# Gate and up of a SwiGLU layer as 2x2 block products, three of eight pairs of k tiles by seven products in place of eight

## The chip, the cores and the metric

The kernel runs on one core of a Trainium2 chip. The metric is device time in microseconds (us) of one execution, as a median of runs. Below, PE is TensorE (matmul), PEld its weight load, DVE is VectorE, ACT is ScalarE, POOL is GpSimd and SP is SyncE, which issues the transfers (DMAs).

## What is computed

The reference is a trunk of two layers over 256 tokens with a width of 2048. Each layer is a mixer (attention and recurrence, or pooling and attention), a residual with layer norm, a SwiGLU feed-forward part of hidden width 5632, and again a residual with layer norm. All is fp32. The change lies in the feed-forward part:

```python
def swiglu(x, w_gate, w_up, w_down):
    return (jax.nn.silu(x @ w_gate) * (x @ w_up)) @ w_down

for layer in range(2):
    y = ab_mixer(x, ...) if layer % 2 == 0 else cd_mixer(x, ...)   # each ends in "@ w_out"
    x = layer_norm(DN_ALPHA * x + y, ln_mix_g[layer], ln_mix_b[layer])
    f = swiglu(x, ffn_w_gate[layer], ffn_w_up[layer], ffn_w_down[layer])
    x = layer_norm(DN_ALPHA * x + f, ln_ffn_g[layer], ln_ffn_b[layer])
```

## The kernel before

**A product in three matmuls.** Every fp32 operand is kept as two parts, high (`h`, `hi`) and low (`l`, `lo`), and a product of a 128x128 piece of x (the stationary operand) with 128 rows by 512 columns of a weight is three matmuls into one bank of PSUM (`mm3`, L240 to L243): low by high, high by high, high by low. The 256 tokens are two tiles of 128, and the contraction over 2048 is 16 k tiles.

**Weights.** They stream in as halves: 128 x 2 k tiles x 512 columns, 512 KB, one DMA on SP's queue into one of four buffers `raw` (`load_half`, L124). ACT copies the high part into `whi` (L103), DVE subtracts it from `raw` and has the low part in `wlo` (L104). `whi` and `wlo` take their slots in turn from a ring: six slots in a pool of their own, and five more in the layer's end (two in a pool `wx`, three in `f0` or `f1`), 11 in all. The two parts of a half feed 12 matmuls: two k tiles, two token tiles, three each.

**The feed-forward part** (`ffn`, L353). The hidden width is 11 chunks of 512. They go in three phases, PHASES = ((0, 1, 2), (3, 4, 5, 6), (7, 8, 9, 10)). In a phase each chunk has eight halves of gate for both token tiles into two banks `acc`, then eight halves of up into two more; ACT takes the silu of gate (`sil`, L367), DVE multiplies it by up (L374), and PE transposes the result in eight pieces (L100) that are split into `yTh` and `yTl` for the next product. Behind the chunks of a phase stand its down products: four column blocks, with DVE adding each into the residual `res` (L257, L259). The residual norm behind the last phase reads `gam` and `bet`, which are loaded (L328, L329) at the start of the feed-forward part.

**The order of the work.** The program is written out as above; a scheduler then fixes the order of every engine when the program is built, with priorities as hints. On the chip each engine works through its order and waits on semaphores. PSUM has eight banks, shared as three `acc`, two `tr` (transposes) and three `mx`.

Of the kernel before, what the change touches and what calls it, by code (L numbers as in the profile page):

```python
# [11 lines left out]
F32 = mybir.dt.float32  # L12
# [58 lines left out]

@with_exitstack
def trunk(ctx: ExitStack, tc: tile.TileContext, a, out):
# [7 lines left out]
    ps = ctx.enter_context(tc.tile_pool(name="ps", bufs=1, space=PSUM))  # L81
# [8 lines left out]
    def acc():  # L90
        return ps.tile([P, NCH], F32, tag="acc", name="acc", bufs=3)

    def trp():
        return ps.tile([P, NCH], F32, tag="tr", name="tr", bufs=2)

    def mxp():
        return ps.tile([P, NCH], F32, tag="mx", name="mx", bufs=3)
# [4 lines left out]
    def split(hi, lo, src):  # L102
        nc.scalar.copy(hi, src)  # L103
        nc.vector.tensor_tensor(lo, src, hi.bitcast(F32), op=sub)  # L104
# [5 lines left out]
    rings = [(wp, 6)]  # L110
# [10 lines left out]
    last_load = [None]  # L121
    first = [True]

    def load_half(src, between=()):  # L124
# [5 lines left out]
        with tc.high_priority(offset=400):  # L130
# [5 lines left out]
            for i in range(parts):  # L136
# [7 lines left out]
                with ExitStack() as order:  # L144
                    for ins in behind:
                        order.enter_context(tc.issue_after(ins))
                    split(hi[:, s, :], lo[:, s, :], raw[:, s, :])
        return hi, lo

    def mm_chunk(halves, lhs, outs, tok_major=False, after=None, before=None):  # L150
# [8 lines left out]
        def mms(i, tok, pin=False):  # L159
            hi, lo = loaded[i]  # L160
            k0 = halves[i][1]
            for kk in range(2):
                xh, xl = lhs(tok, k0 + kk)
# [62 lines left out]
    def transpose4(src, hi, lo):  # L226
# [4 lines left out]
        split(hi, lo, v)  # L231
# [19 lines left out]
    def residual_tools(res, gam, bet, betT):  # L251
        stats = [sm.tile([P, 4, 6], F32, tag=f"st{t}", name=f"st{t}", bufs=1) for t in range(NT)]
# [82 lines left out]
    def out_proj(w, order, groups, res, gb):  # L335
        evac, norm = residual_tools(res, *gb)
        lhs = y_lhs(groups)
        xT = new_xT()
        for n in range(4):
            outs = [acc() for _ in range(NT)]  # L340
            halves = [(w[n, 2 * g + i], 4 * g + 2 * i) for g in order for i in range(2)]
# [11 lines left out]
    def ffn(fp, layer, xT, res, gb, last):  # L353
        evac, norm = residual_tools(res, *gb)
        lhs = x_lhs(xT)
        new = None if last else new_xT
        nxt = [None]
        for pi, chunks in enumerate(PHASES):
            groups = {}
            for c in chunks:  # L360
                first = pi == 0 and c == 0
                gouts = [acc() for _ in range(NT)]
                sil = {}

                def silu(tok):
                    sil[tok] = fp.tile([P, NCH], F32, tag="sil", name="sil", bufs=3)
                    nc.scalar.activation(sil[tok], gouts[tok], AF.Silu)  # L367

                mm_chunk([(a[f"gate{layer}"][c, i], 2 * i) for i in range(8)], lhs, gouts, tok_major=first, after=silu)
                uouts = [acc() for _ in range(NT)]  # L370
                groups[c] = new_yT()

                def gated(tok):
                    nc.vector.tensor_tensor(sil[tok], sil[tok], uouts[tok], op=mult)  # L374
                    s = slice(tok * P, (tok + 1) * P)
                    transpose4(sil[tok], groups[c][0][:, :, s], groups[c][1][:, :, s])

                mm_chunk([(a[f"up{layer}"][c, i], 2 * i) for i in range(8)], lhs, uouts, after=gated)
            end = pi == len(PHASES) - 1
            if end and not last:  # L380
                nxt[0] = new_xT()
            gl = [groups[c] for c in chunks]
            for n in range(4):
                outs = [acc() for _ in range(NT)]
                halves = [(a[f"down{layer}"][n, 2 * c + i], 4 * ci + 2 * i) for ci, c in enumerate(chunks) for i in range(2)]

                def after(tok):
                    with tc.high_priority(offset=1000 if end and n == 3 else 0):
                        evac(tok, n, outs[tok], pi == 0, end)
                        if end and n == 3:  # L390
                            norm(tok, nxt[0], out if last else None)

                mm_chunk(halves, y_lhs(gl), outs, tok_major=(end and n == 3), after=after)
        return nxt[0]
# [29 lines left out]
    def ab_mixer(mp, xT, yT):  # L424
# [239 lines left out]
        for c, ((kind, i), _) in enumerate(ab_plan()):  # L664
            outs = [acc() for _ in range(NT)]
            mm_chunk([(a["ab_in"][c, n], 2 * n) for n in range(8)], lhs, outs, before=load_x if c == 0 else None)
# [5 lines left out]
    def cd_mixer(mp, xT, yT):  # L672
# [118 lines left out]
        for c, (kind, _) in enumerate(cd_plan()):  # L791
            outs = [acc() for _ in range(NT)]
            mm_chunk([(a["cd_in"][c, n], 2 * n) for n in range(8)], lhs, outs, tok_major=(c == 0))
# [10 lines left out]
    with tc.tile_pool(name="ab", bufs=1) as mp:  # L804
        ab_mixer(mp, xT, yT)
# [4 lines left out]
    open_ring(ctx.enter_context(tc.tile_pool(name="wx", bufs=1)), 2)  # L810
    with tc.tile_pool(name="f0", bufs=1) as fp:
        open_ring(fp, 3)
        xT = out_proj(a["ab_out"], AB_OUT_GROUPS, yT, res, load_gb(fp, 0, "mix"))
        xT = ffn(fp, 0, xT, res, load_gb(fp, 0, "ffn"), False)
    rings.pop()
    yT = [new_yT() for _ in range(4)]
    with tc.tile_pool(name="cd", bufs=1) as mp:
        cd_mixer(mp, xT, yT)
    with tc.tile_pool(name="f1", bufs=1) as fp:
        open_ring(fp, 3)  # L820
        xT = out_proj(a["cd_out"], CD_OUT_GROUPS, yT, res, load_gb(fp, 1, "mix"))
        ffn(fp, 1, xT, res, load_gb(fp, 1, "ffn"), True)
# [54 lines left out]

def layout(i):
# [26 lines left out]
    for l in range(2):  # L905
        m[f"gate{l}"] = pieces(f["ffn_w_gate"][l])
        m[f"up{l}"] = pieces(f["ffn_w_up"][l])
# [24 lines left out]
```

## Time and profile before

| | |
|---|---|
| median of 3 runs | 2231.93 us (2229.7 to 2233.01) |
| the profiled execution, its own time | 2229.76 us |
| its span, first to last instruction | 2228.0 us |
| PE busy | 2201.6 us, 99% |
| DVE busy | 1313.6 us, 59% |
| ACT busy | 994.5 us, 45% |
| DMA queue of the weights | 418.94 MB, 57.4% of 16 engines |

The busy time of an engine is the time in which at least one instruction was at work, and says nothing of whether the others waited for it; that is read from the chain that ended last and from the list of waits.

### The profile page before, as it was taken

Reading aid. Unit: us, or ns where it says so; the run is one execution under the profiler, and the core shown is the slowest. Engines: PE = TensorE matmul, PEld = TensorE weight load, DVE = VectorE, ACT = ScalarE, POOL = GpSimd, SP = SyncE. Lnnn points to the kernel's source line nnn. Section 1 sums busy time; section 2 is a strip of 40 time slices with the busy share of each in tenths; the row PEclk is TensorE's granted clock in tenths of the full one; section 3 lists DMA queues with packets and bytes.
Section 4 is the critical chain, followed back from the end, with each engine's and each line's share of the span. In section 5 each row is a group of like instructions: output and inputs, shape, how many; then the busy total and the mean of one; then the engine's idle time right before and its main releaser. Section 6 shows DMA issues by size and latency. Waiting matters only on the chain.

```text
span 2228.0 us, 26810 instructions
## 1 busy us (share of the span) xinstructions
PE 2201.6 (99%) x10180; PEld 1833.9 (82%) x10180; DVE 1313.6 (59%) x1662; ACT 994.5 (45%) x1258; POOL 83.1 (4%) x67
## 2 busy tenths in 40 slices
PE   8999999999999999999999999999999999999997
PEld 7888888887888888888888788878888888888886
DVE  6886688667555545554455676665554554544454
ACT  6445544546443444344443564444444444444431
POOL 0010001002000000000000200020000000000001
PEclk9999999999999999999999999999999999999999
DMA  8555545676655556565656464656555555656562
GB/s 293 161 161 180 173 130 183 219 250 211 205 187 191 190 188 194 184 199 184 197 176 199 151 207 141 235 171 227 188 190 192 186 192 186 198 179 201 183 197 71
DMA packets 118898, 420.66 MB, mean 189 GB/s; under 512 B 14448, under 2 KB 17008, under 8 KB 117488
## 3 DMA queue, kind: packets, MB, share of 16 engines
q1 hardware_dynamic: 118768, 418.94, 57.4%
q8 instruction: 80, 1.31, 0.2%
q14 instruction: 50, 0.41, 0.1%
HBM read 416.78 MB, written 2.10 MB: 188 GB/s over the span
## 4 chain that ended last, share of the span: by engine, by line
PE 96%; DVE 2%; ACT 1%; DMA 0%; issue 0%; POOL 0%; DVEq 0%; ACTq 0%; POOLq 0%
PE acc L243 91%; PE tr L100 2%; PE mx L530 1%; PE mx L243 1%; DVE wlo L104 1%; DVE xTl L319 0%; PE mx L576 0%; PE mx L783 0%; ACT whi L103 0%; ACT res L288 0%; DVE res L274 0%; DMA raw<-in_cd_in 0%; DMA x<-in_xT 0%; DVE res L278 0%; PE mx L766 0%
## 5 line engine op out<-in xcount | busy, mean ns | idle before, releaser
L104 DVE TENSOR_TENSOR wlo<-raw,whi 128x1024 fp32r<-128x1024 f32 (+1 forms) x761 | 938.4, 1236 | 726.2 <-ACT whi L103 708.8
L103 ACT CAST whi<-raw 128x1024 fp32r<-128x1024 f32 (+1 forms) x761 | 800.6, 1053 | 987.4 <-PE acc L243 836.2
L243 PE MATMUL acc<-whi,xTl 128*128 128x512 f32 x2080 | 814.7, 394 | 13.7 <-DVE xTl L319 8.0
L243 PE MATMUL acc<-whi,xTh 128*128 128x512 f32 x2080 | 814.4, 392 | 0.0
L243 PE MATMUL acc<-wlo,xTh 128*128 128x512 f32 x2080 | 808.7, 391 | 0.3 <-DVE wlo L104 0.3
L243 PEld LDWEIGHTS acc<-whi,xTl 128*128 128x128 f32 x2080 | 392.3, 189 | 93.5 <-DVE xTl L319 8.5
L243 PEld LDWEIGHTS acc<-wlo,xTh 128*128 128x128 f32 x2080 | 392.0, 188 | 81.6 <-DVE wlo L104 0.7
L243 PEld LDWEIGHTS acc<-whi,xTh 128*128 128x128 f32 x2080 | 392.4, 189 | 78.5
L243 PE MATMUL acc<-whi,yTl 128*128 128x512 f32 x960 | 375.0, 391 | 0.1
L243 PE MATMUL acc<-whi,yTh 128*128 128x512 f32 x960 | 373.8, 389 | 0.0
L243 PE MATMUL acc<-wlo,yTh 128*128 128x512 f32 x960 | 370.0, 389 | 0.0
L243 PEld LDWEIGHTS acc<-wlo,yTh 128*128 128x128 f32 x960 | 180.2, 188 | 37.8 <-DVE wlo L104 0.4
L243 PEld LDWEIGHTS acc<-whi,yTl 128*128 128x128 f32 x960 | 180.3, 188 | 37.0 <-DVE yTl L789 0.3
L243 PEld LDWEIGHTS acc<-whi,yTh 128*128 128x128 f32 x960 | 180.3, 188 | 36.7
L200 POOL TENSOR_TENSOR rstd<-rstd,mhalf 128x4 f32<-128x4 f32 (+2 forms) x18 | 17.6, 976 | 1799.8 <-DVE rstd L197 1656.9
L104 DVE TENSOR_TENSOR yTl<-tr,yTh 128x512 fp32r<-128x512 f32 x48 | 31.1, 686 | 79.5 <-ACT yTh L103 79.5
L103 ACT CAST yTh<-tr 128x512 fp32r<-128x512 f32 x48 | 26.0, 589 | 94.4 <-PE tr L100 94.3
L320 POOL TENSOR_TENSOR res<-res,bet 128x512 f32<-128x512 f32 x24 | 39.4, 1650 | 26.0 <-PE tr L100 14.6
L259 DVE TENSOR_TENSOR res<-res,acc 128x512 f32<-128x512 f32 x32 | 21.9, 685 | 25.4 <-PE acc L243 24.9
L530 PEld LDWEIGHTS mx<-qq,kk 128*128 128x128 f32 x256 | 33.6, 191 | 2.6
L530 PE MATMUL mx<-qq,kk 128*128 128x128 f32 x256 | 33.8, 274 | 0.0
L257 DVE SCALAR_TENSOR_TENSOR res<-res,acc 128x512 f32<-128x512 f32 x32 | 21.8, 683 | 16.7 <-PE acc L243 15.7
(162 smaller groups left out, 829.4 us busy)
## 6 DMA issues: line engine op xcount, KB each, us to landing
raw<-in_gate SPq DMA_DIRECT2D x176, 512.0 KB, 3.9
raw<-in_up SPq DMA_DIRECT2D x176, 512.0 KB, 4.3
raw<-in_down SPq DMA_DIRECT2D x176, 512.0 KB, 4.1
raw<-in_ab_in SPq DMA_DIRECT2D x127, 512.0 KB, 4.1
raw<-in_cd_in SPq DMA_DIRECT2D x40, 512.0 KB, 4.3
raw<-in_ab_out SPq DMA_DIRECT2D x32, 512.0 KB, 4.7
raw<-in_cd_out SPq DMA_DIRECT2D x32, 512.0 KB, 4.0
x<-in_xT SPq DMA_DIRECT2D x8, 256.0 KB, 6.3
```

What stands on the lines that cost most here:

```text
L100: return nc.tensor.transpose(o, src, eye)
L103: nc.scalar.copy(hi, src)
L104: nc.vector.tensor_tensor(lo, src, hi.bitcast(F32), op=sub)
L200: nc.gpsimd.tensor_tensor(r[:, :n], r[:, :n], mhalf[:, :n], op=ALU.pow)
L243: ins = nc.tensor.matmul(o, lhs[a], rhs[b], start=start and n == 0, stop=stop and n == 2)
L257: nc.vector.scalar_tensor_tensor(r, r, ALPHA, psum, op0=mult, op1=add)
L259: nc.vector.tensor_tensor(r, r, psum, op=add)
L320: nc.gpsimd.tensor_tensor(r, r, bet[:, s], op=add)
L530: nc.tensor.matmul(m[:, 2 * h + s, :], kk[:, h, s * P : (s + 1) * P], qq[:, h, r * P : (r + 1) * P], start=True, stop=True,)
```

## The change

Gate and up of a layer are stored together, by chunk and pair of k tiles (k, k+1): four blocks of 128 x 512, in the order gate k, gate k+1, up k+1, up k (1 MB). Phase one works as before, with halves taken from these. In phases two and three a chunk, now called a unit, has four sums: `c11` (token tile 1, gate), `c12` (tile 1, up), `c21` and `c22` (tile 2). Each pair of k tiles is a 2x2 by 2x2 block product. Five of the eight pairs are done plainly by two halves (eight products). The pairs 5, 6 and 7 (5 and 6 in a phase's last unit) are done by seven products, in Winograd's form of Strassen's scheme: `load_seven` loads the pair's 1 MB by one DMA into the one buffer `rs`, DVE forms four combinations of the four blocks (`z`, three operations of 1024, 512 and 512 elements a partition), and ACT and DVE split the seven operands, 1536 elements of `rs` and 2048 of `z`, into `sh` and `sl` (two buffers each). The forms of x are made once a layer (`forms_of`), while the down products of phase one run. Four further sums p1, p6, p5 and p7 collect the products that several results share; at the unit's end eight DVE operations of 512 elements put gate and up together (L472 to L481), ACT takes the silus, and two products follow (L485). The transposes of a unit are issued two and three halves into the next (`later`).

PSUM is used as two sides of four banks in these phases: one side holds the c sums, the other the p sums, and with each unit the sides change places (`side_bank`). The weight ring has four slots in these phases, 11 in the rest of the layer's end as before (4 + 7; in the last down products 4 + 4 + 3), 6 in the first mixer and 8 in the second, as before. `gam` and `bet` of the feed-forward norm are loaded in the last down products.

The core of the diff:

```diff
+SEVEN = (5, 6, 7)
+PAIRS_FIRST = (0, 1, 2, 3, 5, 4, 6, 7)
+PAIRS = (0, 1, 5, 2, 3, 6, 4, 7)
+PAIRS_LAST = (0, 5, 1, 2, 6, 3, 4, 7)
+BEHIND = (10, 4, 0)
...
-    rings = [(wp, 6)]
+    rings = [(wp, 4)]
...
+    def forms_of(sp, xT, out):
+        n = len(SEVEN)
+        xs = sp.tile([P, NT, 2 * n, P], F32, tag="rs", name="xs", bufs=1)
+        fs = sp.tile([P, 4, n, P], F32, tag="z", name="fs", bufs=1)
+        yield
+        for t in range(NT):
+            s = slice(2 * SEVEN[0], 2 * SEVEN[0] + 2 * n)
+            nc.vector.tensor_tensor(xs[:, t], xT[0][t][:, s, :].bitcast(F32), xT[1][t][:, s, :].bitcast(F32), op=add)
+            yield
+        x11, x12, x21, x22 = (xs[:, t, e : 2 * n : 2, :] for t in range(2) for e in range(2))
+        e, f, g, h = (fs[:, i] for i in range(4))
+        nc.vector.tensor_tensor(e, x22, x21, op=sub)
+        nc.vector.tensor_tensor(f, e, x11, op=add)
+        yield
+        nc.vector.tensor_tensor(g, x11, x21, op=sub)
+        nc.vector.tensor_tensor(h, x12, f, op=sub)
+        yield
+        hi, lo = split_tile(sp, [P, 4, n, P], fs, "fm")
...
+    def load_seven(sp, src, behind):
...
+            raw = sp.tile([P, 4, NCH], F32, tag="rs", name="rs", bufs=1)
+            hi = sp.tile([P, 7, NCH], F32R, tag="sh", name="sh", bufs=2)
+            lo = sp.tile([P, 7, NCH], F32R, tag="sl", name="sl", bufs=2)
+            z = sp.tile([P, 4, NCH], F32, tag="z", name="z", bufs=1)
+            last_load[0] = nc.sync.dma_start(raw, src).ins
+            nc.scalar.copy(hi[:, :3], raw[:, :3])
+            nc.vector.tensor_tensor(z[:, :2], raw[:, 0:3:2], raw[:, 3:4].to_broadcast([P, 2, NCH]), op=add)
+            nc.vector.tensor_tensor(z[:, 2], z[:, 0], raw[:, 2], op=add)
+            nc.vector.tensor_tensor(z[:, 3], z[:, 2], raw[:, 1], op=add)
+            nc.vector.tensor_tensor(lo[:, :3], raw[:, :3], hi[:, :3].bitcast(F32), op=sub)
+            split(hi[:, 3:], lo[:, 3:], z)
...
+    SEVEN_ORDER = ((0, "11", "p1"), (5, "f", "p6"), (3, "e", "p5"), (4, "g", "p7"), (1, "12", "c11"), (2, "h", "c12"), (6, "22", "c21"))
+    def unit(sp, pairs, sevens, w, lhs, forms, yT, opening):
+        b = {n: side_bank() for n in ("c11", "c21", "c12", "c22")}
...
+        behind = [low[-n] if opening and n else None for n in BEHIND]
+        for p in pairs:
+            if p in sevens:
+                if "p1" not in b:
+                    b.update((n, side_bank(True)) for n in ("p1", "p6", "p5", "p7"))
+                wt = load_seven(sp, w[p], behind.pop(0))
+                for i, x, name in SEVEN_ORDER:
+                    product(name, forms[p][x], wt(i))
+            else:
+                for n, ks in ((0, (2 * p, 2 * p + 1)), (1, (2 * p + 1, 2 * p))):
+                    hi, lo = load_half(w[p][:, 2 * n : 2 * n + 2])
+                    for tok in range(NT):
+                        for kk in range(2):
+                            product(f"c{tok + 1}{n + 1}", lhs(tok, ks[kk]), (hi[:, kk, :], lo[:, kk, :]))
+                    half_done()
+        with tc.high_priority(offset=1000):
+            g0, w_, v, x = (sp.tile([P, NCH], F32, tag=n, name=n, bufs=1) for n in ("g0", "g1", "u0", "u1"))
+            nc.scalar.copy(g0, b["p1"])
+            nc.vector.tensor_tensor(w_, g0, b["p6"], op=sub)
+            nc.vector.tensor_tensor(v, w_, b["p5"], op=add)
+            nc.vector.tensor_tensor(w_, w_, b["p7"], op=add)
+            nc.vector.tensor_tensor(x, w_, b["p5"], op=add)
+            nc.vector.tensor_tensor(g0, g0, b["c11"], op=add)
+            nc.scalar.activation(g0, g0, AF.Silu)
+            nc.vector.tensor_tensor(v, b["c12"], v, op=sub)
+            nc.vector.tensor_tensor(w_, w_, b["c21"], op=add)
+            nc.scalar.activation(w_, w_, AF.Silu)
+            nc.vector.tensor_tensor(x, b["c22"], x, op=sub)
+            banks["side"] ^= 1
+            for tok, (g, u) in enumerate(((g0, v), (w_, x))):
+                nc.vector.tensor_tensor(g, g, u, op=mult)
+                s = slice(tok * P, (tok + 1) * P)
+                later.append([2 + tok, lambda g=g, s=s: transpose4(g, yT[0][:, :, s], yT[1][:, :, s], 1000)])
```

Over the whole program the order of PE has 8988 matmuls of 512 columns where there were 9120, and as many transposes as before (176 behind gate and up); the loads of gate and up go from 352 halves to 264 halves and 44 transfers of 1 MB.

Three places in the built program, engine by engine. Numbers behind a name tell buffers apart. First DVE in phase two before: the splits of a chunk's halves, the two products of gate and up, the splits of the transposed result, and the next chunk.

```order
L104 TENSOR_TENSOR wlo<-raw,whi 128x1024 x15
L374 TENSOR_TENSOR sil<-sil,acc 128x512 x2
L104 TENSOR_TENSOR wlo<-raw,whi 128x1024
L104 TENSOR_TENSOR yTl<-tr,yTh 128x4x128 x2
L104 TENSOR_TENSOR wlo<-raw,whi 128x1024 x15
```

And DVE after the change, where unit 4 (the second of phase two in the first layer) goes over to unit 5. `rs_6545`, `sh_6546` and `sl_6547` are pair 7 of unit 4; just ahead of the first row stands `sl_6547<-rs_6545` (L434, 1536 elements), the last reading of that `rs`. `rs_6691` is pair 5 of unit 5, `wlo_6646` and `wlo_6671` its halves of pair 1; `bside_6368`, `bside_6369` and `bside_6370` are p6, p5 and p7 of unit 4.

```order
L128 TENSOR_TENSOR sl_6547<-z_6548,sh_6546 128x2048
L431 TENSOR_TENSOR z_6694<-rs_6691 128x1024
L128 TENSOR_TENSOR wlo_6646<-raw_6644,whi_6645 128x1024
L432 TENSOR_TENSOR z_6694<-z_6694,rs_6691 128x512
L434 TENSOR_TENSOR sl_6693<-rs_6691,sh_6692 128x1536
L433 TENSOR_TENSOR z_6694<-z_6694,rs_6691 128x512
L128 TENSOR_TENSOR wlo_6671<-raw_6669,whi_6670 128x1024
L472 TENSOR_TENSOR g1_6579<-g0_6578,bside_6368 128x512
L473 TENSOR_TENSOR u0_6580<-g1_6579,bside_6369 128x512
L476 TENSOR_TENSOR g0_6578<-g0_6578,aside_6277 128x512
L128 TENSOR_TENSOR sl_6693<-z_6694,sh_6692 128x2048
L474 TENSOR_TENSOR g1_6579<-g1_6579,bside_6370 128x512
```

The recombination of unit 4 (L472 to L474) now stands behind the whole preparation of unit 5's first seven; before, the two products of gate and up followed a split directly.

PE at the same place: before, the matmuls of the next chunk go on around the eight transposes, in other banks.

```order
L243 MATMUL acc<-whi,xTl_3812 128x512
L243 MATMUL acc<-whi,xTh_3810 128x512
L100 MATMUL tr<-ident,sil 128x128 x8
L243 MATMUL acc<-whi,xTl_3813 128x512
L243 MATMUL acc<-whi,xTh_3811 128x512
L243 MATMUL acc<-wlo,xTh_3811 128x512
```

After the change, the first 30 matmuls of unit 5 go into `bside_6597` (c11) and `bside_6598` (c21), 15 each; these are the last of them and the first of `c12`, `bside_6599`, which takes the bank that was p7 of unit 4.

```order
L283 MATMUL bside_6598<-wlo_6646,xTh1_3815 128x512
L283 MATMUL bside_6598<-sh_6692,xTl1_3817 128x512
L283 MATMUL bside_6598<-sh_6692,xTh1_3815 128x512
L283 MATMUL bside_6598<-sl_6693,xTh1_3815 128x512
L283 MATMUL bside_6599<-whi_6620,xTl0_3816 128x512
L283 MATMUL bside_6599<-whi_6620,xTh0_3814 128x512
L283 MATMUL bside_6599<-wlo_6621,xTh0_3814 128x512
```

What moved is the order within a unit: the halves and the first seven of unit 5 are used for gate first, for both token tiles, and `c12` begins when the bank of p7 is free.

SP issues the loads. Before, they are halves alone:

```order
L140 DMA raw<-in_down 128x1024 x24
L140 DMA raw<-in_gate 128x1024 x8
L140 DMA raw<-in_up 128x1024 x8
L140 DMA raw<-in_gate 128x1024 x8
L140 DMA raw<-in_up 128x1024 x8
```

After, at the same boundary as above, from the first half of unit 5 (`raw_6601`) on:

```order
L429 DMA rs_6545<-in_gu0 128x2048
L166 DMA raw_6601<-in_gu0 128x1024
L166 DMA raw_6619<-in_gu0 128x1024
L166 DMA raw_6644<-in_gu0 128x1024
L166 DMA raw_6669<-in_gu0 128x1024
L166 DMA raw_6724<-in_gu0 128x1024
L166 DMA raw_6742<-in_gu0 128x1024
L429 DMA rs_6691<-in_gu0 128x2048
L166 DMA raw_6760<-in_gu0 128x1024
L429 DMA rs_6796<-in_gu0 128x2048
```

Six halves now stand between the loads of pair 7 of unit 4 and of pair 5 of unit 5, and `raw_6760` stands behind the latter.

## Rows read from the trace of the kernel before

**Rows 1.** The page: span, busy time, granted clock in tenths, shares of the chain.
```profile
span 2228.0 us, 26810 instructions
PE 2201.6 (99%) x10180; PEld 1833.9 (82%) x10180; DVE 1313.6 (59%) x1662; ACT 994.5 (45%) x1258; POOL 83.1 (4%) x67
PEclk9999999999999999999999999999999999999999
PE 96%; DVE 2%; ACT 1%; DMA 0%; issue 0%; POOL 0%; DVEq 0%; ACTq 0%; POOLq 0%
```

**Rows 2.** Waits of PE: what for, us in all, times, longest.
```profile
PE acc L243 <- DVE xTl L319: 8.0, 2, 4.0
PE acc L243 <- DVE xTl L104: 5.7, 1, 5.7
...
PE acc L243 <- DVE wlo L104: 0.3, 1, 0.3
```

**Rows 3.** The chain in phase two of the first layer: start us, us, what.
```profile
767.06 43.55 PE acc L243 x192
810.61 0.87 PE tr L100 x8
```

**Rows 4.** Windows: down of phase one, phase two's chunks, down of phase two.
```profile
core 0: us, PE busy (x) PEld busy (x) DVE busy (x) ACT busy (x) POOL busy (x), PEclk, DMA share, GB/s
657.30:722.70 65.40, 65.40 (x290) 54.14 (x289) 35.84 (x34) 26.05 (x26) 0.00 (x0) 1.00 0.57 191
722.80:900.30 177.50, 177.50 (x801) 147.34 (x800) 87.43 (x78) 75.48 (x79) 0.00 (x0) 1.00 0.58 190
900.30:987.40 87.10, 87.10 (x386) 72.11 (x385) 45.64 (x42) 34.49 (x34) 0.00 (x0) 1.00 0.59 192
```

**Rows 5.** Groups of phase two's chunks: busy us, mean ns, idle before and releaser.
```profile
L104 DVE TENSOR_TENSOR wlo<-raw,whi 128x1024 fp32r<-128x1024 f32 x64 | 78.4, 1225 | 78.7 <-ACT whi L103 77.3
L103 ACT CAST whi<-raw 128x1024 fp32r<-128x1024 f32 x64 | 67.5, 1055 | 87.1 <-PE acc L243 76.6 <-issue 10.5
...
L374 DVE TENSOR_TENSOR sil<-sil,acc 128x512 f32<-128x512 f32 x8 | 5.5, 684 | 0.1
L367 ACT ACTIVATE sil<-acc 128x512 f32<-128x512 f32 x8 | 4.8, 595 | 2.1 <-PE acc L243 2.1
...
L104 DVE TENSOR_TENSOR yTl<-tr,yTh 128x512 fp32r<-128x512 f32 x6 | 3.9, 687 | 10.5 <-ACT yTh L103 10.5
L103 ACT CAST yTh<-tr 128x512 fp32r<-128x512 f32 x7 | 3.8, 589 | 16.6 <-PE tr L100 16.6
```

**Rows 6.** Timeline of DVE, three stretches: start us, us, instruction, idle before it.
```profile
93.92 1.22 DVE L104 TENSOR_TENSOR wlo<-raw,whi 128x1024 fp32r<-128x1024 f32 x1
95.04 0.42 DVE L566 TENSOR_TENSOR Pf<-Pf 128x256 f32<-128x256 f32 x1
95.38 0.42 DVE L549 TENSOR_TENSOR kk<-kf,Qf 128x256 f32<-128x256 f32 x1
...
499.83 0.69 DVE L261 BATCH_NORM_STATS2 st<-res 128x6 f32<-128x512 f32 x1
500.55 0.26 DVE L265 BATCH_NORM_AGGREGATE mv<-st 128x2 f32<-128x24 f32 x1
...
511.79 0.67 DVE L257 SCALAR_TENSOR_TENSOR res<-res,acc 128x512 f32<-128x512 f32 x1
512.38 0.60 DVE L319 SCALAR_TENSOR_TENSOR xTl<-tr,betT,xTh 128x128 fp32r<-128x128 f32 x2
```

**Rows 7.** Groups of loads: KB each, median us from issue to landing.
```profile
raw<-in_down SPq DMA_DIRECT2D x176, 512.0 KB, 4.1
```

**Rows 8.** The loads of the feed-forward part's `gam`: issues, landing.
```profile
L328 SPq DMA_DIRECT2D gam<-in_ln_ffn_g x2: 328/328/328, 517.6 to 1485.9; - x2
...
DMA to landing us min/median/max: 4.6/5.8/7.0
```

**Rows 9.** The loads of the residual `res`: issues, landing.
```profile
L809 SPq DMA_DIRECT2D res<-in_x x2: 327/380/433, 433.4 to 433.7; - x2
...
DMA to landing us min/median/max: 7.6/8.6/9.6
```

More of the change, by code (lines that the diff above doesn't have):

```diff
@@ L121, in trunk @@
     last_load = [None]
+    low = []
     first = [True]
@@ L248, in at, with new_stats, residual_tools @@
         return pair[0][ix], pair[1][ix]
-    def residual_tools(res, gam, bet, betT):
-        stats = [sm.tile([P, 4, 6], F32, tag=f"st{t}", name=f"st{t}", bufs=1) for t in range(NT)]
+    def new_stats():
+        return [sm.tile([P, 4, 6], F32, tag=f"st{t}", name=f"st{t}", bufs=1) for t in range(NT)]
+    def residual_tools(res, gam, bet, betT, stats):
         def evac(tok, n, psum, start, last):
@@ L340, in out_proj @@
             outs = [acc() for _ in range(NT)]
-            halves = [(w[n, 2 * g + i], 4 * g + 2 * i) for g in order for i in range(2)]
+            halves = [(w[n, 2 * g + i], two(4 * g + 2 * i)) for g in order for i in range(2)]
             def after(tok):
@@ L358, in ffn @@
         for pi, chunks in enumerate(PHASES):
-            groups = {}
+            end = pi == len(PHASES) - 1
             for c in chunks:
[L361 to L378, printed above, removed]
@@ L379, in ffn @@
-            end = pi == len(PHASES) - 1
-            if end and not last:
-                nxt[0] = new_xT()
-            gl = [groups[c] for c in chunks]
+                if pi == 0:
+                    groups[c] = whole(c, mix_pool, c == 0)
+                else:
+                    groups[c] = new_yT()
+                    pairs = PAIRS_FIRST if c == chunks[0] else PAIRS_LAST if c == chunks[-1] else PAIRS
+                    sevens = SEVEN[:-1] if c == chunks[-1] else SEVEN
+                    unit(sp, pairs, sevens, w[c], lhs, forms, groups[c], c == chunks[0])
@@ new lines, in ffn @@
+            if pi == 0:
+                close_mix()
+                sp = later_pool(stack, f"sp{layer}")
+                open_banks("sides")
+                making.append(forms_of(sp, xT, forms))
+                later.append([2, make])
+            gl = [groups[c] for c in chunks]
+            if end:
+                stack.close()
+                open_banks("uses")
+                open_ring(keep(f"er{layer}"), 4)
+                open_ring(later_pool(stack, f"e{layer}"), 3)
+                fp = later_pool(stack, f"g{layer}")
+                nxt = None if last else new_xT()
@@ L383, in ffn @@
+            stats = new_stats()
+            evac, norm = residual_tools(res, None, None, None, stats)
             for n in range(4):
+                if end and n == 1:
+                    evac, norm = residual_tools(res, *load_gb(fp, layer, "ffn"), stats)
                 outs = [acc() for _ in range(NT)]
-                halves = [(a[f"down{layer}"][n, 2 * c + i], 4 * ci + 2 * i) for ci, c in enumerate(chunks) for i in range(2)]
+                halves = [(a[f"down{layer}"][n, 2 * c + i], two(4 * ci + 2 * i)) for ci, c in enumerate(chunks) for i in range(2)]
@@ L390, in after @@
                         if end and n == 3:
-                            norm(tok, nxt[0], out if last else None)
+                            norm(tok, nxt, out if last else None)
                 mm_chunk(halves, y_lhs(gl), outs, tok_major=(end and n == 3), after=after)
-        return nxt[0]
+            if not end:
+                banks["side"] ^= 1
+        if end:
+            rings.pop()
+            stack.close()
+        return nxt
     def attend(pool, probs, v_of):
```

136 lines of the change are left out of this document (104 added, 32 removed).

## The prediction

> **What bounds the kernel now.** I read the page first [rows 1]: TensorE (PE) is busy 2201.6 of 2228.0 us, VectorE (DVE) 59% and ScalarE (ACT) 45%, and the chain that ended last is 96% PE. The clock row holds 9 throughout, so the clock is not what moves. Next, what PE waits for [rows 2]: 8.0 and 5.7 us of its idle time lie behind the normalisations (`xTl`), and 0.3 us behind one weight (`wlo`). In the feed-forward part PE waits for nothing: the chain in the second phase [rows 3] is one chunk after another, 43.55 us of 192 matmuls and 0.87 us of eight transposes. The pitch of a matmul is thus 43.55 / 192 = 0.2268 us. The windows say how much room the others have [rows 4]: while PE is busy for all 177.5 us of phase two's four chunks, DVE works 87.4 and ACT 75.5 us, and the transfers take 58% of their engines at 190 GB/s. The change is worth what it takes off PE, as long as DVE, which gets the additions, keeps up.
>
> **What goes from PE.** A pair of k tiles for two token tiles and for gate and up is eight products of three matmuls; seven products are one product less. Phases two and three hold eight units (chunks) in each layer; six take three pairs by seven and two (the last of a phase) take two: 6x3 + 2x2 = 22, in both layers 44. 44 x 3 = 132 matmuls go, which is the difference that the order of PE shows (9120 to 8988 of 512 columns), the others unchanged: 132 x 0.2268 = **29.9 us**. A unit with three sevens is then 183 x 0.2268 + 0.87 = 42.4 us, a last unit 186 x 0.2268 + 0.87 = 43.1 us.
>
> **What DVE gets.** An operation now takes 1.225 us for 1024 elements and 0.684 to 0.687 us for 512, one source in PSUM or not [rows 5]. Back to back they stand closer [rows 6]: the next starts 1.12 us after one of 1024, 0.59 after one of 512, 0.34 after one of 256; an operation that needs the result of the last starts 0.03 us behind its end (499.83 + 0.69 to 500.55). A further 512 elements cost 1.12 - 0.59 = 0.53, so 1536 are 1.65 and 2048 are 2.18 us (estimates; nothing of that size is in the trace). One seven is 1.12 + 2 x 0.59 + 1.65 + 2.18 = 6.13 us. A unit has three (18.4), ten halves (11.2), and twelve operations of 512 (eight of recombination, two gate times up, two splits of the transposed result: 7.1): **36.7 us** of PE's 42.4; the last unit 12 x 1.12 + 2 x 6.13 + 7.1 = 32.8 of 43.1. Now it is 87.43 / 4 = 21.9 a chunk. With full durations, nothing overlapping, a seven is 1.225 + 2 x 0.685 + 1.765 + 2.305 = 6.67, and the unit 20.0 + 12.25 + 8.2 = 40.5 us. I take the first, since the rows that show operations standing together all show the overlap; the other end is a rival.
>
> **ACT** has per unit ten copies of 1.055, three each of 1536 and 2048 (1.52 and 1.99 by the slope 1.055 - 0.589), and about five of 0.6 [rows 5]: 10.6 + 10.5 + 3 = 24 of 42.4. Transfers: the same bytes in 42.4 in place of 44.4 us, 190 to 199 GB/s, share 0.61. Neither is near its end.
>
> **The x forms** are made once a layer: two operations of 768, four of 384, a split of 1536, by the same slope about 0.86 x 2 + 0.46 x 4 + 1.65 = 5.2 us on DVE, in the down products of phase one, where DVE works 35.8 of 65.4 us [rows 4]. Nothing; without that cover 5 us a layer.
>
> **The transfer of 1 MB.** The pairs by seven come through one buffer, `rs`: SP issues the next transfer when DVE has read the last, and the halves issued after it stand behind it in SP's queue. Such a load is not in the trace; halves of 512 KB land 4.1 us after issue [rows 7] and the nearest of 1 MB, among halves of weights as here, is `gam` of the feed-forward part: 4.6 and 7.0, median 5.8 [rows 8]. The upper end is `res`, 7.6 and 9.6 [rows 9]; it goes with `gam` and `bet` of the mixer straight behind it, which these loads do not have. I take 5.8. DVE's own work between its last reading of one `rs` and its first addition from the next covers it: along its order 6.2, 6.7 and 2.2 to 3.3 us, about 15.5 in a unit. At 5.8 DVE waits 3 x 5.8 - 15.5 = 1.9, 36.7 + 1.9 = 38.6 of 42.4; at 7.0 it is 42.2, still within.
>
> **The handover between units.** This is where I expect PE to wait. PSUM is now two sides of four banks, and the first matmuls of a unit overwrite banks whose p products DVE must have read. At the boundary of units 4 and 5 (C is PE's start of unit 5, the chain followed along the orders): the half 0b of unit 5 (`whi_6620`) takes the slot that PE releases 66 matmuls ahead, C - 15.0. ACT copies it (1.05) and behind it does the 1536 copy of `rs_6545` into `sh_6546` (1.5): C - 12.4. DVE subtracts (L434, 1.65 and 0.03 behind the copy): C - 10.7, which frees `rs`; `rs_6691` lands at C - 4.9. DVE then has, in the order shown, 1.12 + 1.12 + 0.59 + 1.65 + 0.59 + 1.12 + 0.59 + 0.72 (it needs the one before) + 0.59 + 2.18 + 0.59 = 10.9 to the end of L474, at C + 6.0. This frees p7's bank for `c12` (`bside_6599`), which PE reaches after 30 matmuls, at C + 6.8. The margin is 0.8 us; at a landing of 7.0 PE waits 0.4. L475, four operations on, frees the bank of `c22`. The other boundaries have 2.5 to 3.6 us, counted in the same way: the tight one occurs once in a phase, four times in all. I put 4 x 0.5 = 2 us on these.
>
> Of two operations that follow each other the rows show an overlap of 0.09 to 0.10 us (93.92 + 1.22 against 95.04) [rows 6]. The Trainium skill, "VectorE: DVE Perf Modes", section "The DRAIN you can't avoid", has the next operation wait until the pipe of the last is empty, and excepts one that is not held; the rows are of the excepted kind. Were all of them held, the chain above would be 12 x 0.09 = 1 us longer, and PE would wait at four places for 0.3 us; what it would do to the unit is rival A.
>
> **The rest at nothing or little.** The ring has 4 slots in place of 11 in phases two and three: a half is used for 12 matmuls, 2.72 us, and 4 slots are 10.9 us ahead, against a conversion of 1.05 + 1.2 us; without that cover, 2.3 us at a place. `gam` and `bet` of the last norm load some 60 us before use. Pools that wait for single tiles, rings that close and open: 1 us in all (from 0 to 5.7, the wait at a norm in [rows 2]).
>
> **Sum.** 29.9 - 2 - 1 = 27. The profiled execution took 2229.8 us (span 2228.0), 2.2 under the median of the runs: 2202.8 profiled, **2205** as a median. A change of 0.2% (4.5 us) is about what a measurement of this kernel tells from none.
>
> **Rivals.**
> A, DVE becomes the bound. By full durations the unit is 40.5, and with 1.5 to 3 of waits for `rs` about 43.9: 1.5 us over PE's 42.4, in 12 units 18, and the gain is 27 - 18 = 9: **2223**. For it: waits of an operation for ACT's copy or for PSUM stand before many operations here, and now DVE idles 78.7 us "behind ACT" [rows 5], so that its overlap is hardly seen in this stage. Against it: the rows that are back to back. The skill's rule above gives the same number if every operation is held. Chance 0.18.
> B, slower: the load through the one `rs` takes as long as `res` [rows 9]. At landing L the unit is 36.7 + 3L - 15.5; it reaches 42.4 at 7.1, and the gain of 27 is gone at 42.4 + 27/12 = 44.65, that is **L = 7.8**. At 8.6 it is 47.0, 12 x 4.6 = 55 us lost: **2260**; at 9.6, 2296. Against it: it needs two or more loads in front of it, and the halves wait for slots that come free one by one. Chance 0.08.
> C, no change: some of both, or waits of 1.7 us in each of 16 units, as when a half comes late behind an operation of 2.2 us. **2232**. Chance 0.07.
> The forecast, 2198 to 2211: 0.67.
>
> The range of 8 in 10 goes from 2198 (no wait anywhere is 2231.9 - 29.9 = 2202; 4 less is about the spread of the runs before, 2229.7 to 2233.0) to 2222, which takes most of A. Faster 0.85 (forecast and A), same 0.07, slower 0.08.
>
> **What the profile would show.** PE: 132 matmuls fewer at the same 0.227 us, units of 41.5 us and 0.87. DVE: 37 to 39 us busy or less in 42.4, and its idle time before `z` (L431) put down to the load. PE's waits: L474 and L475 at the start of the second unit of a phase, about 2 us in sum. `rs` lands in 5 to 7 us. Wrong if DVE's windows are full (A), if landing is above 7.1 (B), or if PE waits for `wlo` in the middle of units (C: the ring).

## The result: 2212.4 us, and the profile after

| | before | changed |
|---|---|---|
| median | 2231.51 us (2229.70 to 2233.01, 4 runs) | 2212.44 us (2209.09 to 2216.94, 4 runs) |
| ratio to before, 95% interval | | 0.9916 [0.9893, 0.9939] |
| profiled execution, its span | 2229.76, 2228.0 us | 2216.94, 2215.2 us |

The kernel became 19.1 us faster. The forecast was 2205, a gain of 27; the time lies in its range (2198 to 2222), and some 8 us of the gain are missing. The page of the changed kernel, beside [rows 1]:

```profile
span 2215.2 us, 26628 instructions
PE 2180.2 (98%) x10048; PEld 1808.4 (82%) x10048; DVE 1558.5 (70%) x1936; ACT 1051.9 (47%) x1276; POOL 82.3 (4%) x67
PEclk9999999999999999999999999999999999999999
rs<-in_gu SPq DMA_DIRECT2D x44, 1024.0 KB, 6.7
```

PE has 132 instructions less (10180 to 10048), DVE 245 us more work, and the loads of 1 MB took 6.7 us. The waits of PE, beside [rows 2] (us in all, times, longest):

```profile
PE acc L283 <- DVE xTl L361: 8.0, 2, 4.0
PE acc L283 <- DVE xTl L128: 5.8, 1, 5.8
PE bside L283 <- DVE sl L128: 2.7, 2, 1.5
PE aside L283 <- DVE sl L128: 2.4, 2, 1.2
PE mx L283 <- DVE ptl L128: 1.2, 1, 1.2
...
PE bside L283 <- ACT g L471: 0.5, 2, 0.4
PE aside L283 <- DVE yTl L128: 0.5, 1, 0.5
```

The first two are those of before. New are four waits for `sl`, the low part of a first seven, and one for `ptl` in the second mixer, where the edit changes how the pool is opened and no line of the work. The windows of two middle units, beside [rows 4] (us, then busy us of PE, PEld, DVE, ACT, POOL, clock, DMA share, GB/s):

```profile
763.40:805.40 42.00, 42.00 (x191) 34.77 (x190) 34.24 (x36) 21.12 (x21) 0.00 (x0) 1.00 0.52 177
805.40:847.10 41.70, 41.70 (x189) 34.35 (x187) 36.24 (x36) 22.67 (x21) 0.00 (x0) 1.00 0.58 203
```

PE is busy throughout, and DVE works 34.2 and 36.2 us where the prediction had 36.7. So the missing microseconds do not stand inside the units. Where they stand shows on the timelines around PE's start of unit 6, the last of phase two (C = 847.2). First PE (start us, us, instruction, idle before it):

```profile
852.35 0.39 PE L283 MATMUL aside<-sh,xTh 128*128 128x512 f32 x1
853.91 0.50 PE L283 MATMUL aside<-sl,xTh 128*128 128x512 f32 x1 [1.17 <-DVE sl L128]
```

ACT's copy of the last `rs` of unit 5, on ACT's timeline:

```profile
834.40 1.48 ACT L430 CAST sh<-rs 128x1536 fp32r<-128x1536 f32 x1 [1.89 <-PE aside L283]
```

SP's issue of the first `rs` of unit 6:

```profile
837.71 0.33 SPq L429 DMA_DIRECT2D rs<-in_gu  x1
```

And DVE, from its last reading of the one to the bank of p7:

```profile
835.92 1.76 DVE L434 TENSOR_TENSOR sl<-rs,sh 128x1536 fp32r<-128x1536 f32 x1 [1.66 <-ACT sh L430]
...
844.30 1.23 DVE L431 TENSOR_TENSOR z<-rs 128x1024 f32<-128x1024 f32 x1 [2.33 <-DMA rs<-in_gu]
845.56 0.69 DVE L432 TENSOR_TENSOR z<-z,rs 128x512 f32<-128x512 f32 x1
...
851.57 2.29 DVE L128 TENSOR_TENSOR sl<-z,sh 128x2048 fp32r<-128x2048 f32 x1
853.77 0.68 DVE L474 TENSOR_TENSOR g<-g,aside 128x512 f32<-128x512 f32 x1
```

Read backwards: PE stands from 852.6 to 853.9 for the 2048 operation of DVE (851.57 to 853.86), the last of a run that began when `rs` landed (844.2). That load was issued 0.03 us after L434 had read the old `rs` (835.92 + 1.76 = 837.68). L434 waited for ACT's copy, and the copy for PE to release a slot of `sh`. This is the chain of the prediction with three things moved: it bites at the last boundary of a phase, not at 4 to 5; what PE meets first is `sl`, ahead of the bank of L474; and it starts at a slot of `sh`.

### The profile page after: what moved, and what is told of

It is laid out like the page before. It is cut to its first block, busy times and chain, and to the rows that moved or that the text cites. A ratio compares the mean times of both kernels' runs of the same rounds, so it can differ in the third digit from the quotient of the medians.

```text
span 2215.2 us, 26628 instructions
## 1 busy us (share of the span) xinstructions
PE 2180.2 (98%) x10048; PEld 1808.4 (82%) x10048; DVE 1558.5 (70%) x1936; ACT 1051.9 (47%) x1276; POOL 82.3 (4%) x67
## 5 line engine op out<-in xcount | busy, mean ns | idle before, releaser
L283 PE MATMUL acc<-whi,xTl 128*128 128x512 f32 x1056 | 418.6, 398 | 14.0 <-DVE xTl L361 8.0
L283 PE MATMUL acc<-whi,xTh 128*128 128x512 f32 x1056 | 417.0, 395 | 0.0
L283 PE MATMUL acc<-wlo,xTh 128*128 128x512 f32 x1056 | 413.4, 394 | 0.3 <-DVE wlo L128 0.3
L283 PEld LDWEIGHTS acc<-whi,xTl 128*128 128x128 f32 x1056 | 200.5, 190 | 54.8 <-DVE xTl L361 8.5
L283 PEld LDWEIGHTS acc<-wlo,xTh 128*128 128x128 f32 x1056 | 200.3, 190 | 41.6 <-DVE wlo L128 0.7
L283 PEld LDWEIGHTS acc<-whi,xTh 128*128 128x128 f32 x1056 | 200.6, 190 | 39.1
L283 PE MATMUL acc<-whi,yTl 128*128 128x512 f32 x512 | 200.5, 392 | 0.1
L283 PE MATMUL acc<-whi,yTh 128*128 128x512 f32 x512 | 199.6, 390 | 0.0
L283 PE MATMUL acc<-wlo,yTh 128*128 128x512 f32 x512 | 197.7, 390 | 0.0
L283 PE MATMUL aside<-whi,xTl 128*128 128x512 f32 x336 | 131.6, 392 | 0.4 <-DVE g L472 0.2
```

Source lines behind the costliest of these rows:

```text
L283: ins = nc.tensor.matmul(o, lhs[a], rhs[b], start=start and n == 0, stop=stop and n == 2)
```

## Experiments

Each kernel was timed in five rounds beside the kernel before; the ratio is to that one.

**1. The changed kernel again** (no edit).

> The changed kernel, timed again beside the others. If the waits in its trace are its own and not an accident of one execution, the same six places come back, with about 8 us of PE's waits at the handovers between units, and the median lies between 2209 and 2215 us, 17 to 22 us under the kernel before. If they were an accident, they are gone, and the time is near the forecast 2205.

2212.18 us, 0.9916 [0.9903, 0.9930]. In phases two and three of the first layer PE waits at the same boundaries for the same operations:

```profile
PE bside L283 <- DVE sl L128: 1.2, 1, 1.2
PE aside L283 <- DVE sl L128: 1.2, 1, 1.2
PE aside L283 <- ACT g L471: 0.4, 1, 0.4
PE bside L283 <- ACT g L471: 0.2, 1, 0.2
```

The waits are the kernel's own. Their size varies: in the second layer this execution lost 4.1 us in phases two and three, the profiled one above 5.8 (by the method of run 2).

**2. The rest of the change without the sevens.**

```diff
...
-                    unit(sp, pairs, sevens, w[c], lhs, forms, groups[c], c == chunks[0])
+                    groups[c] = whole(c, sp, False)
...
```

The forms of x go with it.

> Layout, PSUM sides, ring of four slots and late norm weights as in the changed kernel, but every unit by plain products: 9120 matmuls of 512 columns, as before. The forecast put all these edits at 1 us: then it runs within 0.1% of the kernel before (2230 to 2234). The rival is that the missing 8 us of the gain lie here (a ring with too few slots, PSUM pools that open late): then 2238 to 2242, and PE waits for wlo inside the units.

2236.83 us, 1.0025 [1.0014, 1.0035], 5.5 us over the kernel before. Neither branch as it stood: the rest costs far more than 1 us, but PE waits for no `wlo` inside the units. I added up, over PE's rows of the timeline, what lies between two starts beyond 0.2268 us for a matmul of 512 columns (0.1134 for 256, 0.109 for a transpose):

| stretch, us | before | plain units | changed (run 1) | two `rs` (run 7) |
|---|---|---|---|---|
| 0 to 545: mixer, out projection, norm | 11.6 | 13.3 | 13.1 | 12.4 |
| 545 to 715: phase one and its down | 0.0 | 0.8 | 0.8 | 0.6 |
| 715 to 1160: phases two and three | 0.0 | 0.0 | 4.7 | 0.5 |
| 1160 to 1480: last down, norm, second mixer | 7.3 | 9.7 | 9.2 | 10.1 |
| 1480 to 1640: norm, phase one, layer 2 | 6.9 | 8.5 | 7.3 | 6.6 |
| 1640 to the end: phases two and three, layer 2 | 0.0 | 0.5 | 4.1 | 0.4 |
| sum | 25.8 | 32.9 | 39.3 | 30.5 |

So the ring of four slots costs nothing that can be seen (third and last rows). Of the 7.1 us between the first two sums, 1.7 lie in the first stretch, and those are the execution's and not the edit's: over all the kernels here this stretch goes from 11.5 to 14.7. Up to 20 us, at the start, 2.4 and 3.5 us are lost; from 515 to 545, around the first norm, 6.0 and 6.7. There PE waits 4.0 us, and behind the wait the granted clock is 0.50 (1.2 GHz) from 529.3 to 532.5 us in the trace of before and from 527.7 to 534.3 in that of run 2. The other 5.4 us agree with the medians' 5.5 and lie outside the units of phases two and three. Some 3.3 us stand where the PSUM sides open or close: 0.8 (645 to 660 us), 0.6 (1155 to 1175), 1.4 (1600 to 1640) and 0.5 (from 2080 on). Another 1.5 us lie in the second mixer, from 1300 to 1480. There the waits of PE between 1160 and 1480 us have one more than before:

```profile
PE mx L283 <- DVE ptl L128: 1.2, 1, 1.2
PE tr L124 <- ACT res L330: 1.2, 1, 1.2
PE acc L283 <- DVE wlo L128: 0.3, 1, 0.3
```

The order of PE in that mixer is another one in the changed program (the transposes of `rx` and the products with `dkTh` stand elsewhere among the halves); that this order, or the pool that now waits for single tiles, costs the 1.5 us was not tried alone.

**3. The first seven later in the last unit.**

```diff
-PAIRS_LAST = (0, 5, 1, 2, 6, 3, 4, 7)
+PAIRS_LAST = (0, 1, 2, 5, 3, 6, 4, 7)
```

> One line: the last unit of a phase takes its first pair by seven as the fourth of eight pairs in place of the second. If PE's waits stand at the handover because the load of 1 MB for the first seven comes late, four of the six places (about 6.5 of 8 us) lose their wait: 5 to 6 us under the changed kernel, about 2207. If VectorE is the bound, the wait only moves, and the time stays within 1 us.

2214.23 us, 0.9925 [0.9912, 0.9937]: not faster. The wait for `sl` is gone in the first layer, and in its place stands another of the same size:

```profile
PE aside L283 <- DVE g L474: 1.2, 1, 1.2
PE bside L283 <- DVE g L474: 1.2, 1, 1.2
PE bside L283 <- ACT g L471: 0.5, 1, 0.5
```

This is the wait of the prediction, `c12` for the bank that L474 frees. L474 stands behind the `sl` operation in DVE's order, so a need moved back meets the same late chain there. By the table's method phases two and three lose 6.1 us in the first layer (4.7 in run 1) and 1.4 in the second (4.1), together 1.3 less, and the stretches outside them were 2.3 more in this execution. Four places should have lost 6.5 us; the theory that the place of the first seven alone is at fault falls.

**4. More work for DVE.**

```diff
             split(hi[:, 3:], lo[:, 3:], z)
+            nc.vector.tensor_tensor(z[:, :2], z[:, :2], z[:, :2], op=add)
```

> One more DVE operation of 1024 elements for every seven (an addition into z that nobody reads), 1.13 us back to back, 3.4 us in a unit with three sevens, 50 us in the whole program. If DVE has the room that the overlapping durations give it (36.7 + 3.4 + waits for rs of 42.4), the time rises by 0 to 8 us, from longer chains at the handovers alone. If DVE is the bound (rival A), nearly all of it shows: 20 to 45 us slower than the changed kernel.

2212.73 us, 0.9918 [0.9905, 0.9932]: no slower, with 44 more operations of 1.22 us. DVE is busy 38.60 and 36.86 us in the two middle units, and PE all of them (42.00 and 41.70 us). The waits at the handovers have other names in the new order (`whi` four times 0.9 us, `sl` four times 0.2), and by the table's method phases two and three lose 4.1 us in each layer where run 1 lost 4.7 and 4.1: the extra work is not hidden behind a smaller handover. At three sevens DVE has that much room: rival A is not what happened.

**5. The first seven later in every unit but a phase's first.**

```diff
-PAIRS = (0, 1, 5, 2, 3, 6, 4, 7)
-PAIRS_LAST = (0, 5, 1, 2, 6, 3, 4, 7)
+PAIRS = (0, 1, 2, 5, 3, 6, 4, 7)
+PAIRS_LAST = (0, 1, 2, 5, 3, 6, 4, 7)
```

The reason to try it is in the order of PE. In unit 5 the seven products of pair 5 (`sh_6692`) begin 12 matmuls into the unit, but the last of them, p7, stands 124 matmuls in, behind the first products of pair 6 (`sh_6797`). The numbers in front are places in the built order, where four transposes are one place:

```
3367 L283 MATMUL bside_6597<-sh_6692,xTl0_3816 128x512
3445 L124 MATMUL aside_6662<-ident_72,g1_6579 128x128 x4
3477 L283 MATMUL aside_6689<-sh_6797,fml_5834 128x512
3481 L283 MATMUL aside_6690<-sh_6692,fml_5834 128x512
```

Its bank `aside_6690` is the one that the second transpose, `aside_6662`, holds until DVE has read it. In the trace DVE has read it at 830.8 and PE comes to p7 at 833.8, the place that its order gives it. Until p7 is done the slot of `sh` is taken, and ACT's copy for pair 7 waits: the 1.89 us at 834.40 above.

> The first pair by seven is the fourth of eight in every unit of a phase but the first, not only in the last. In the built order the last product (p7) of a unit's first seven then stands 113 matmuls into the unit and not 127, so the slot of sh that it holds comes free 3 us earlier, and with it the copy that frees rs for the next unit. If that chain (p7's bank, held by the second transpose, then the slot of sh, the copy, rs, the load, DVE) sets the wait, the waits at the handovers, 4 to 6 us, go: about 2208. If DVE's own work behind the load sets it (as L474 did when only the last unit was moved), the time stays at 2212 to 2214.

2208.13 us, 0.9894 [0.9877, 0.9910]: 4 us under the changed kernel, as the first branch had it (counted from the unit's first matmul the product p7 stands at 110 and 124, not 113 and 127; the difference is the same 14, or 3.2 us). The waits at the handovers, in the first layer alone, are

```profile
PE aside L283 <- DVE g L474: 0.9, 1, 0.9
PE bside L283 <- DVE g L474: 0.7, 1, 0.7
```

The edit moves the release and the need together; run 3, which moved the need in the last unit alone, gave nothing, so the release counts. The loads landed sooner too (5.9 us in the median), which this run does not separate.

**6. Three ring slots, the control for the next two.**

```diff
-    rings = [(wp, 4)]
+    rings = [(wp, 3)]
...
-        rings.append((wab, 2))
+        rings.append((wab, 3))
...
-        open_ring(later_pool(stack, f"fr{i}"), 7 - 4 * i)
+        open_ring(later_pool(stack, f"fr{i}"), 8 - 4 * i)
...
-                open_ring(keep(f"er{layer}"), 4)
+                open_ring(keep(f"er{layer}"), 5)
```

> Control for the next two: the weight ring has three slots in place of four in phases two and three (one slot more in the mixers' rings, so that these have as many or one more than before). If the ring still covers the conversion (three halves are 8.2 us), 0 to 3 us slower than the changed kernel. If the ring is already what PE waits for, 10 us or more slower, with waits for wlo inside the units.

2211.13 us, 0.9912 [0.9897, 0.9926]: no slower. PE's waits in phases two and three are then for `whi` in part (1.7 us, the longest). It is not the slots that set this one but again the load: ACT stands for `rs`, copies it, and only then comes to the half that PE needs.

```profile
1072.77 1.47 ACT L430 CAST sh<-rs 128x1536 fp32r<-128x1536 f32 x1 [4.05 <-DMA rs<-in_gu]
1074.15 1.04 ACT L127 CAST whi<-raw 128x1024 fp32r<-128x1024 f32 x1
...
1075.24 0.50 PE L283 MATMUL aside<-whi,xTl 128*128 128x512 f32 x1 [1.73 <-ACT whi L127]
```

The one `rs` thus reaches PE by two ways, through DVE's order and through ACT's.

**7. Two buffers `rs`**, on the control.

```diff
-        xs = sp.tile([P, NT, 2 * n, P], F32, tag="rs", name="xs", bufs=1)
+        xs = sp.tile([P, NT, 2 * n, P], F32, tag="rs", name="xs", bufs=2)
...
-            raw = sp.tile([P, 4, NCH], F32, tag="rs", name="rs", bufs=1)
+            raw = sp.tile([P, 4, NCH], F32, tag="rs", name="rs", bufs=2)
```

> The control with two buffers rs in place of one. If the single rs sets the wait at the handover, DVE's 39 us of waits for the load fall under 10, PE's waits for sl, L471 and L474 at the handovers fall under 2 us, and the time is 4 to 6 us under the control. If DVE or the banks set it, DVE waits elsewhere and the time is within 1 us of the control.

2204.86 us (2204.69 to 2206.76), 0.9883 [0.9868, 0.9897]: 6.3 us under the control, 7.3 under the changed kernel. In phases two and three PE waits for nothing at all in either layer. The instructions that use `rs`, what the engines waited for before them, and the landing:

```profile
  DMA rs<-in_gu: 2.0, 2
...
DMA to landing us min/median/max: 4.6/6.7/8.6
```

In the changed kernel the same two lines are

```profile
  DMA rs<-in_gu: 82.1, 47
...
DMA to landing us min/median/max: 4.6/6.7/8.2
```

In the control the waits for `rs` are 104.2 us in 58 places, the landing 6.8 in the median. The loads take as long as before, only nobody waits for them. By the table's method phases two and three lose 4.8 and 2.1 us in the control and 0.5 and 0.4 here: 6.0 of the 6.3 us, with the same three slots. The single `rs` made the handovers late.

**8. Four of eight pairs by seven**, on the control.

```diff
-SEVEN = (5, 6, 7)
-PAIRS_FIRST = (0, 1, 2, 3, 5, 4, 6, 7)
-PAIRS = (0, 1, 5, 2, 3, 6, 4, 7)
+SEVEN = (4, 5, 6, 7)
+PAIRS_FIRST = (0, 1, 2, 4, 5, 3, 6, 7)
+PAIRS = (0, 4, 1, 5, 2, 6, 3, 7)
...
-                    sevens = SEVEN[:-1] if c == chunks[-1] else SEVEN
+                    sevens = SEVEN[1:-1] if c == chunks[-1] else SEVEN
```

> The control with four of eight pairs by seven (three in a phase's last unit): 60 sevens in place of 44, 48 matmuls less, 10.9 us of PE. DVE's unit is 4 x 6.13 + 8 x 1.12 + 7.1 = 40.6 of PE's 41.7 us, and the waits for the one rs come on top (4 loads of 6.7 against some 16 to 18 us of other work). If DVE's sum holds, DVE becomes the bound here: 15 to 60 us slower than the control. If DVE still has room, 5 to 11 us faster than the control.

As built a last unit keeps two sevens: 56 in all, 36 matmuls or 8.2 us less of PE, not 10.9. 2303.11 us, 1.0323 [1.0308, 1.0339]: 92 us slower than the control, and worse than the expectation's upper end. Two stretches of about one unit each, windows:

```profile
770.00:818.00 48.00, 42.49 (x180) 32.55 (x181) 38.06 (x37) 22.62 (x20) 0.00 (x0) 1.00 0.51 175
818.00:866.00 48.00, 42.48 (x176) 33.78 (x175) 42.19 (x40) 23.58 (x21) 0.00 (x0) 0.93 0.48 175
```

DVE's waits in the first of them:

```profile
DVE sl L128 <- ACT sh L127: 5.1, 3, 2.0
DVE z L431 <- DMA rs<-in_gu: 3.5, 3, 1.5
DVE g L472 <- PE bside L283: 0.6, 1, 0.6
DVE sl L434 <- ACT sh L430: 0.5, 2, 0.3
```

And in the second:

```profile
DVE z L431 <- DMA rs<-in_gu: 3.6, 4, 1.6
DVE sl L128 <- ACT sh L127: 0.8, 2, 0.6
```

In the first 38.1 us of work and 9.9 of waits fill the 48.0 us, in the second 42.2 and 5.8: DVE is never free. Over both windows the load takes 7.1 us of the waits and `sl`'s wait for ACT's copy of `z` 5.9, up to 2.0 us a time, which the sum did not have. The mean work of the two units, 40.1, is the 40.6 of the sum.

**9. Two `rs` and the first seven later** (the edits of 5 and 7).

> Three ring slots and two buffers rs, and besides the later place of the first seven. With two rs PE's trace shows no wait at a handover, so a later place has nothing left to give: within 1.5 us of the kernel with two rs alone (2204.9), 2203 to 2207. If a hidden part of the handover is left (matmuls at the lower clock behind short waits), 2 us or more faster.

2210.26 us, 0.9906 [0.9892, 0.9920]: 5.4 us slower than with two `rs` alone (5.1 by the ratios), against both branches. The trace has four new waits, one in each phase, at the second unit's start:

```profile
PE bside L283 <- ACT whi L127: 1.9, 2, 1.0
PE aside L283 <- ACT whi L127: 1.9, 2, 1.0
```

They are 3.8 of the 5.4 us. With the first seven behind three plain pairs a unit begins with six halves, through three slots; ACT's copy in front of the first of these waits had itself waited 0.35 us for PE, as it would for a slot in use; that the slots are the cause was not tried.

**10. Two `rs` and much more work for DVE.**

```diff
             split(hi[:, 3:], lo[:, 3:], z)
+            nc.vector.tensor_tensor(z, z, z, op=add)
```

> Two rs, and one more DVE operation of 2048 elements for every seven: 2.18 us back to back, 6.5 us in a unit. By the sum of overlapped durations DVE's unit is 36.7 + 6.5 = 43.2 of PE's 42.4: 0.8 us over in 12 units, 10 us, and some more at the handovers: 2213 to 2225. By full durations (40.5 + 6.9 = 47.4) it is 5 us over in 12 units: 2260 or more. If DVE has more room than either sum says, 2205.

2263.77 us, 1.0145 [1.0131, 1.0159]: 59 us slower than run 7, the time of the sum by full durations, but not for its reason. The window of one unit as DVE goes (from one L473, which is L472 of the changed kernel, to the next):

```profile
810.50:861.50 51.00, 45.35 (x191) 35.88 (x191) 44.38 (x41) 22.89 (x21) 0.00 (x0) 0.97 0.49 165
```

DVE's waits there:

```profile
DVE sl L128 <- ACT sh L127: 4.0, 2, 2.0
DVE wlo L128 <- ACT whi L127: 1.5, 3, 1.0
DVE sl L434 <- ACT sh L430: 1.2, 1, 1.2
```

44.4 of work (the sum was 43.2, with overlap) and 6.7 of waits for ACT make the 51.0. As in run 8 the sum lacks DVE's standing in its order for ACT.

**11. Three ring slots, plain units** (the edits of 2 and 6).

> The kernel with three ring slots with every unit by plain products (no sevens; the same 9120 matmuls of 512 columns as before). If the layout, the PSUM sides and the pools cost 5.5 us in this form too, as with four slots, 2235 to 2238; the sevens with two rs then give more than their 29.9 us, which would need another cause. If this form costs 2 to 4 us, 2233 to 2236, and the ledger of the kernel with two rs closes.

2236.80 us, 1.0026 [1.0017, 1.0036]: the first branch. Between this and run 7 the sevens give 31.9 us where 29.9 were counted. By the table's method the two executions differ by 2.7 us beside the matmuls (33.2 and 30.5 in sum), 1.6 of them in the first stretch; the 2.0 of the medians are within the medians' intervals, 2 to 3 us.

**12. Two `rs`, and the PSUM sides opened later.**

```diff
-                open_banks("sides")
...
-            if not end:
+            if pi == 0:
+                open_banks("sides")
+            elif not end:
                 banks["side"] ^= 1
```

> The kernel with three ring slots and two rs; the two PSUM sides are opened behind the down products of phase one in place of ahead of them. In the trace of the kernel with two rs PE loses 0.6 and 0.9 us where these products begin (the pools' banks are handed over there). If the handing over costs this, it goes, or moves to the start of phase two: between 2203 and 2205 in time, which the timing hardly tells from 2204.9, so the verdict is the trace's: excess under 0.2 us at both places. If the loss has another cause (the transposes that wait for DVE's product), it stays.

2209.67 us, 0.9902 [0.9885, 0.9918], 4.8 us slower than run 7 (4.2 by the ratios, whose intervals overlap). The excess where the down products begin falls to 0.0 us at both places, and at the start of phase two PE now waits for the last read of the old banks, in the first layer

```profile
PE aside L283 <- DVE res L299: 0.9, 1, 0.9
```

and as long in the second. So the handing over of the banks costs about 1 us wherever it stands. The rest was not followed; by the table's method the two executions differ by 5.7 us, 1.6 of it from 715 to 1160 us (2.1 against 0.5), 3.2 from 1640 on (3.6 against 0.4) and 1.3 ahead of 545 (13.7 against 12.4), the stretch that varies by itself.

## Why the prediction was right, and where its sum was off

The time lies in the range, and the wait that was named is the one that was found. By the number alone it stands 1.4 us above the forecast's own interval (2198 to 2211), on the side of rival A; that A is not what happened is read from DVE's windows and run 4. Two terms were too small, and nothing made up for them: the handovers by 3.2 us and the pools by 4.5, together 7.7 of the 7.9 that are missing.

**PE's saving** held: 132 instructions less, and the pitch stayed (852.12 to 852.35, 0.23 us).

**DVE's price** held. The 36.7 us of a unit are 34.2 and 36.2 in the trace; the unseen sizes stand as estimated: a 2048 operation is followed after 2.20 us (851.57 to 853.77; estimate 2.18), and one that needs the result of the last 0.03 us behind its end (844.30 + 1.23 to 845.56). The Trainium skill, "VectorE: DVE Perf Modes", section "The DRAIN you can't avoid", gave rival A's time for operations that are all held; in this trace the start stands 0.09 us before the end of the last, as in [rows 6], so these operations are of the kind that the section excepts, and run 4 took 44 more operations for nothing. What the step left out is DVE's wait for ACT within a seven, up to 2.0 us a time, when DVE has no room left (runs 8 and 10). At three sevens there is room; with one seven more in a unit, or one more operation of 2048 elements in each seven, DVE does become the bound, and what it stands for ACT and the load then costs more than what its work exceeds PE's.

**The load**, sized by `gam` [rows 8] at 5.8, took 6.7 in the median and up to 8.2: nearer to `res` [rows 9] than I took it. Rival B's point, 7.8, was passed by single loads and not by their median. `res` itself took 5.8 in the median in the changed kernel's trace, so the upper end of the prediction was one execution's.

**The handover** was the right mechanism with a wrong size: 2 us in the sum; by the medians of runs 1 and 2 (24.7 of the sevens' 29.9 us arrive) it is 5.2, by the two traces of the table 8.8 (4.7 + 4.1 against 0.0 + 0.0). I had one tight boundary in a phase with 0.8 us of margin. The trace has it at the last boundary, where the first seven is the second pair and `sl` is needed 24 matmuls in, and where the copy that frees `rs` waits for a slot of `sh`; there the margin is -1.3. I had counted the need of L474's bank and left out that of `sl`. Two `rs` remove nearly all of it (run 7, 0.9 left), an earlier release most (run 5), a later need alone next to nothing (run 3).

**"Pools, rings: 1 us"** was the other step that failed: 5.5 us (run 2). The ring, which I had in mind, costs nothing; the opening and closing of the PSUM sides goes with some 3.3 us in the trace of run 2, and 1.5 lie in the second mixer, whose cause stays open. The term's range, from 0 to 5.7, held by luck: its upper end was read as the wait at a norm, but the 5.7 us of [rows 2] are PE's wait at the start of the program, whose first matmul begins at 5.66 us; only the two waits of 4.0 us stand at the norms. The medians make 29.9 - 5.5 - 5.2 = 19.2, which closes by itself, since both terms are differences of the same medians; the traces make 2228.0 - 29.9 + (39.3 - 25.8) = 2211.6, by the way of counting nearly the span of run 1 (2211.4).

**The x forms, the late `gam` and `bet`** show nothing: no wait of PE names them.

## What to carry to other kernels

A unit of work that is saved on the busiest engine arrives only if the next unit's operands do: follow the first operand of the next unit back through its buffers, and count for every tile on the way who releases it and when, with the built order at hand, not the written one. A single buffer in front of a load of 6 to 8 us cost more here than 44 needless operations on the engine that was feared for. And price a layout change outside its own stage too: the same change with the gain taken out is one run, and it found 5.5 us where the sum had 1.

## What the runs showed of the hardware

An engine that is 79% busy can set the time: in the first window of run 8 DVE works 38.1 of 48.0 us and stands the rest in its order, nearly all of it for a copy or a load.

Where PE had stood long, its granted clock was lower for a while. In run 10 PE waits 6.1 us, until 870.05; the windows around it (columns as in [rows 4]):

```profile
867.00:873.00 6.00, 2.95 (x7) 2.40 (x8) 6.00 (x11) 2.40 (x2) 0.00 (x0) 0.50 0.38 104
874.00:910.00 36.00, 36.00 (x165) 29.73 (x163) 28.87 (x27) 17.62 (x18) 0.00 (x0) 1.00 0.54 180
```

0.50 is the lower of its two levels (1.2 and 2.4 GHz). In the units of the changed kernel, whose waits are of 1 us, it stays at 1.00. Behind the waits of 4.0 us at the norms it is at 0.50 for 3.2 us at some and for over 6 at others, the trace of before having one of each; from 1480 to 1600 us run 1 (short) lost 5.9 us by the table's method and run 2 (long) 7.1, so that this alone moves an execution by about 1 us.

Loads of the same 1 MB took 4.6 to 8.6 us in one kernel (run 7).
